# Block sums of w_up formed by GpSimd at three stretches of the front and stored, and the down stage's loads and last round in another order

## The chip, the cores and the metric

The kernel runs on one core of one Trainium2 chip. The time is the device time of one execution in microseconds (us); lower is better. Below, PE is TensorE, DVE is VectorE, ACT is ScalarE, POOL is GpSimd, and SP is SyncE, which here only issues DMAs.

## The reference

One decoder layer on x of 1024 tokens by 1024 channels, everything in float32:

```
h = RMSNorm(x);  z = h @ W_in            (pool | q | k | v | sgu u, v | three gates)
branches: pooling mixer, banded attention, chunked spatial gating, each projected to 1024
x = x + (sum_i sigmoid(gate_i) * branch_i) @ W_out
h = RMSNorm(x);  up = h @ W_up           (1024 x 5632: the first 2816 columns gate, the rest val)
up = causal depthwise conv of width 3;   x = x + (silu(gate) * val) @ W_down     (2816 x 1024)
```

The change touches the product with W_up, the product with W_down, and what runs beside the work ahead of them.

## The kernel before

**Products.** Each float32 operand is split into a high and a low part of a rounded type (fp32r): ACT copies the high part (helper line 86), DVE subtracts it from the source for the low part (line 87). One product is then three matmuls, high by high, high by low, low by high (helper `three`, lines 173 to 175). `clock` adds up the nominal time of the matmuls written so far; generators in `tasks` and similar lists are stepped as it goes on, and a scheduler of the builder then sets each engine's order from modelled durations. SP's queue of DMA issues is in order, like every engine's.

**Front (0 to about 655 us).** It runs for two halves of the tokens, t = 0 and t = 1. A half takes x in, normalises it, multiplies by the columns of W_in for keys and values, queries and gating, runs the attention, then goes through the `units` (the gated branches, whose partial sums stand in the big tile `part`), and ends with W_out. Four tiles called `x2` hold rows of x for the residual.

**Up stage (about 655 to 1103 us).** W_up's columns are taken in 22 groups c of 128 gate and 128 val columns. A group's product is made by a block scheme with seven products P1 to P7 where a plain 2 by 2 scheme has eight. The halves of the input dimension and the gate and val columns give the blocks a11, a12 (gate) and a21, a22 (val). The weights of P3, P5, P6 and P7 are sums of blocks: s1 = a21+a22 (P5), s2 = s1-a11 (P6), s3 = a11-a21 (P7), s4 = a12-s2 (P3). `up_prep` loads g and v of a group (512 KB each) into `raw` slots, POOL forms the four sums in two `q` slots (lines 858 to 861, four operations of 128x512 each), and ACT and DVE split each of the seven weights. For groups 0 to 6 P1 and P2 are done early (set PRE) and the other five products (REST) in the up stage; groups 7 to 21 do all seven there (FULL). The evacuation of a group (conv, silu, gate by val) runs on DVE and ACT, its long operation being line 875 (128x1023). The `q` slots (13 of 128x1024) are shared by sums, split weights and evacuation.

**Down stage (about 1103 us to the end).** The 22 groups are taken as 11 pairs q, in two parts (q 0 to 5, then 6 to 10), again with seven products each by blocks A11 to A22 of the gated activations (`gd`, in DRAM) and B11 to B22 of W_down. `fetch` loads the blocks of a part in a written order. Each product has four PSUM banks (i = 0 to 3); `evacuate` combines them on DVE and ACT, either at the product's last step or later (list `late`, one product on). Finished tiles are added into `out` in DRAM by accumulating DMAs that POOL issues (`add`, line 1045); the last product's tiles are stored by SP (line 1080). In the last part the order of products ends P7, P5, P4, and P5 releases eight tiles (v2 and v3, four each) to `add`. In this stage the orders of DVE and ACT are as written.

Of the kernel before, what the change touches and what calls it, by code (L numbers as in the profile page):

```python
# [35 lines left out]
LOADS, READY = 9, 7  # L36


def trunk_kernel(tc, x, positions, norm1, w_in, q_norm, k_norm, sinks, w_pool, pool_scale,
# [105 lines left out]

    def tick():
        again = True
# [22 lines left out]

    def three(ps, a, b, first, last, n=T):

        pe.matmul(ps, a(0), b(0), start=first, stop=False)  # L173
        pe.matmul(ps, a(0), b(1), start=False, stop=False)  # L174
        r = pe.matmul(ps, a(1), b(0), start=False, stop=last)  # L175
        clock[0] += 3 * n * 0.216 / 512
        return r
# [427 lines left out]

    def up_early(c):
# [33 lines left out]
    gd = [dp.tile([P, S], F32, name=f"gd{c}") for c in range(NC_FF)]  # L640
    mark = [None]
    spawn(setup_rest(), 24)
    st = Stream(w_in, 768, 256, KD, normed.ins)
    for t in range(2):
# [31 lines left out]
        part = slot("part", 1, [P, KD, T], F32)  # L676
# [34 lines left out]
        for i, c0 in enumerate(units):  # L711
            if i + 1 < len(units):
                wn = w_gran(w_in, units[i + 1])
            else:
                x2t = [slot("x2" if t == 0 else "x", 4, [P, D], F32) for _ in range(NT)]
# [31 lines left out]
        ss = slot("ssx", 2, [P, 32], F32)[:, 0:8]  # L747
        if t == 0:
# [88 lines left out]
    def up_prep(c, names):  # L837


        ws = wss[c, names]  # L840
        g = up_raw(0, c)
# [6 lines left out]
        v = up_raw(1, c)  # L848
# [5 lines left out]
        a11, a12, a21, a22 = g[:, 0:HK, :], g[:, HK:, :], v[:, 0:HK, :], v[:, HK:, :]  # L854
        sa, sb = q_([P, 2, HK, P]), q_([P, 2, HK, P])
        s1, s2, s3, s4 = sa[:, 0], sa[:, 1], sb[:, 0], sb[:, 1]
        yield
        pool.tensor_tensor(s1, a21, a22, ALU.add)  # L858
        pool.tensor_tensor(s2, s1, a11, ALU.subtract)
        pool.tensor_tensor(s3, a11, a21, ALU.subtract)  # L860
        pool.tensor_tensor(s4, a12, s2, ALU.subtract)
        for n in names:
            wt = slot("w", 4, [P, 2, HK, P], F32R) if n in ("P1", "P6", "P2") else q_([P, 2, HK, P], F32R)
            ws[n] = up_split({"P1": a11, "P2": a12, "P3": s4, "P4": a22, "P5": s1, "P6": s2, "P7": s3}[n], wt)
# [118 lines left out]
    ORDERS = ("P1", "P2", "P6", "P3", "P7", "P4", "P5"), ("P1", "P2", "P6", "P3", "P7", "P5", "P4")  # L983
# [17 lines left out]
    def fetch(a, b):  # L1001
        for j, q in enumerate(range(a, b)):
            raws[q] = slot("hh", 2, [P, 8, T], F32) if j in (0, 2) else h_([P, 8, T])
            load(q, (A11, B11, A12, B21))
        for q in range(a, b):
            load(q, (A21, B12, A22, B22))
# [40 lines left out]
    def evacuate(part, p, i, ps):  # L1047


        state = states[part]  # L1050
        s, v2, v3, p3 = (state[n][i] for n in ("s", "v2", "v3", "p3"))
        over = lambda v: dve.scalar_tensor_tensor(v, v, -1.0, ps, ALU.mult, ALU.add)
# [8 lines left out]
        elif p == "P3":  # L1061
# [130 lines left out]
```

## Time and profile before

| | us |
|---|---|
| median of 3 runs | 1324.67 (1323.91 to 1326.77) |
| the profiled execution, own time | 1327.64 |
| its span | 1325.9 |
| PE busy | 1285.3 |
| DVE busy | 974.4 |
| ACT busy | 607.8 |
| POOL busy | 189.5 |

The profiled execution is 2.97 us above the median; 1.74 us of its time lie outside the span. Busy shares are means over stages: PE is at 97%, so what can be gained is in the stretches where it is not.

### The profile page before, as it was taken

How to read it: one execution, taken by the hardware profiler on the slowest of the kernel's cores; microseconds unless marked ns; L12 is line 12 of the kernel's file. 1: busy time of each engine (PE TensorE's matmuls, PEld its weight loads, DVE VectorE, ACT ScalarE, POOL GpSimd, SP SyncE). 2: the span in 40 equal slices, each digit the busy share in tenths (PEclk: the TensorE clock that was granted, in tenths of full speed). 3: DMA queues.
4: the chain of work that ended last, by engine and by line, in shares of the span. 5: the costliest groups of instructions: out<-in, count | busy, mean ns of one | idle time of the engine just before them, and what ended most of it. 6: DMA issues, size and time to landing. Idle time of an engine off the chain costs nothing.

```text
span 1325.9 us, 16088 instructions
## 1 busy us (share of the span) xinstructions
PE 1285.3 (97%) x5956; PEld 1064.1 (80%) x5956; DVE 974.4 (73%) x1520; ACT 607.8 (46%) x990; POOL 189.5 (14%) x123
## 2 busy tenths in 40 slices
PE   6999999999999999999999999999999998999996
PEld 6888888888888888888777878878778787788885
DVE  6887875644569776355585889889998885986986
ACT  5655554333465455333573444344444343444441
POOL 0000000000000000000005454245443400101202
PEclk9999999999999999999998999999999999999999
DMA  6422224422432222533554323333232256238705
GB/s 233 118 87 64 80 80 143 115 75 94 148 118 64 81 80 79 152 113 111 200 169 139 104 71 112 112 96 111 81 111 95 80 185 243 48 107 248 122 0 96
DMA packets 167644, 151.25 MB, mean 114 GB/s; under 512 B 7615, under 2 KB 132493, under 8 KB 167565
## 3 DMA queue, kind: packets, MB, share of 16 engines
q1 hardware_dynamic: 163533, 142.87, 33.9%
q0 software_dynamic: 4032, 7.34, 3.7%
q8 instruction: 47, 0.77, 0.2%
q14 instruction: 32, 0.26, 0.1%
HBM read 120.30 MB, written 29.88 MB: 113 GB/s over the span
## 4 chain that ended last, share of the span: by engine, by line
issue 53%; PE 19%; DVE 14%; DMA 5%; ACT 4%; POOL 0%; SPq 0%; POOLq 0%; DVEq 0%; ACTq 0%
DVE x L875 6%; PE bk L1129 4%; PE bk L1128 4%; PE bk L1130 4%; DVE q L87 3%; DMA raw<-in_w_up_dram 3%; PE bk L898 2%; PE bk L899 2%; PE bk L900 2%; ACT x L871 2%; DMA hq<-in_w_down_dram 1%; DVE w L87 1%; ACT w L86 1%; ACT x L883 1%; DVE x L87 1%
## 5 line engine op out<-in xcount | busy, mean ns | idle before, releaser
L175 PE MATMUL mm<-hh,w 128*128 128x512 f32 x416 | 162.6, 391 | 0.0
L173 PE MATMUL mm<-hh,w 128*128 128x512 f32 x416 | 162.6, 391 | 0.0
L174 PE MATMUL mm<-hh,w 128*128 128x512 f32 x416 | 162.4, 390 | 0.0
L87 DVE TENSOR_TENSOR w<-raw,w 128x1024 fp32r<-128x1024 f32 (+1 forms) x96 | 93.3, 976 | 89.5 <-ACT w L86 89.5
L858 POOL TENSOR_TENSOR q<-raw 128x512 f32<-128x512 f32 x22 | 35.6, 1617 | 847.4 <-DVE w L87 653.0
L86 ACT ACTIVATE w<-raw 128x1024 fp32r<-128x1024 f32 (+1 forms) x96 | 82.3, 858 | 155.8 <-PE mm L174 67.1
L875 DVE SCALAR_TENSOR_TENSOR x<-q,cA,x 128x1023 f32<-128x1023 f32 x88 | 136.2, 1554 | 22.8 <-ACT x L871 22.3
L898 PE MATMUL bk<-hq,q 128*128 128x512 f32 x352 | 139.2, 396 | 6.1 <-DVE sm L916 5.9
L899 PE MATMUL bk<-hq,q 128*128 128x512 f32 x352 | 138.0, 392 | 0.0
L900 PE MATMUL bk<-hq,q 128*128 128x512 f32 x352 | 137.6, 391 | 0.0
L1129 PE MATMUL bk<-x,w 128*128 128x512 f32 x308 | 121.1, 393 | 2.5 <-DVE x L87 2.5
L1130 PE MATMUL bk<-w,x 128*128 128x512 f32 x308 | 120.6, 392 | 0.0
L1128 PE MATMUL bk<-w 128*128 128x512 f32 x308 | 93.4, 391 | 4.1 <-ACT w L86 3.8
L174 PEld LDWEIGHTS mm<-hh,w 128*128 128x128 f32 x416 | 78.1, 188 | 16.1
L175 PEld LDWEIGHTS mm<-hh,w 128*128 128x128 f32 x416 | 78.1, 188 | 16.1
L173 PEld LDWEIGHTS mm<-hh,w 128*128 128x128 f32 x416 | 78.1, 188 | 15.7
L87 DVE TENSOR_TENSOR wa<-raw,wa 128x512 fp32r<-128x512 f32 x72 | 49.5, 695 | 55.5 <-ACT wa L86 55.5
L898 PEld LDWEIGHTS bk<-hq,q 128*128 128x128 f32 x352 | 66.6, 189 | 24.4 <-DVE sm L916 8.5
L871 ACT ACTIVATE x<-q,cA 128x1024 f32<-128x1024 f32 x44 | 54.0, 1241 | 68.7 <-DVE q L926 38.0
L86 ACT ACTIVATE wa<-raw 128x512 fp32r<-128x512 f32 x72 | 45.2, 631 | 79.5 <-PE mm L175 67.2
L900 PEld LDWEIGHTS bk<-hq,q 128*128 128x128 f32 x352 | 66.7, 189 | 14.0
L899 PEld LDWEIGHTS bk<-hq,q 128*128 128x128 f32 x352 | 66.7, 189 | 13.7
(267 smaller groups left out, 2957.6 us busy)
## 6 DMA issues: line engine op xcount, KB each, us to landing
raw<-in_w_in_dram SPq DMA_DIRECT2D x72, 512.0 KB, 3.8
raw<-in_w_up_dram SPq DMA_DIRECT2D x51, 512.0 KB, 5.2
gd<-x SPq DMA_DIRECT2D x22, 512.0 KB, 2.8
x<-in_x_dram SPq DMA_DIRECT2D x16, 512.0 KB, 4.0
raw<-in_w_out_dram SPq DMA_DIRECT2D x16, 512.0 KB, 3.7
hq<-gd SPq DMA_DIRECT2D x28, 256.0 KB, 5.3
hq<-in_w_down_dram SPq DMA_DIRECT2D x28, 256.0 KB, 5.6
raw<-in_w_proj_b_dram SPq DMA_DIRECT2D x32, 128.0 KB, 2.7
```

Of the source, the lines that this page charges most:

```text
L86: split.last = act.activation(hi, src, AF.Copy).ins
L87: dve.tensor_tensor(lo, src, f(hi), ALU.subtract)
L173: pe.matmul(ps, a(0), b(0), start=first, stop=False)
L174: pe.matmul(ps, a(0), b(1), start=False, stop=False)
L175: r = pe.matmul(ps, a(1), b(0), start=False, stop=last)
L875: dve.scalar_tensor_tensor(y[:, n:], u[:, 0 : S - n], col(w), y[:, n:], ALU.mult, ALU.add)
L898: pe.matmul(ps, ws[n][:, 0, k, :], rhs[n](0, k), start=start and k == 0, stop=False, skip_group_check=True)
L899: pe.matmul(ps, ws[n][:, 0, k, :], rhs[n](1, k), start=False, stop=False, skip_group_check=True)
L900: pe.matmul(ps, ws[n][:, 1, k, :], rhs[n](0, k), start=False, stop=k == HK - 1, skip_group_check=True)
L1128: pe.matmul(ps[i], hi[:, 0, ts], hi[:, 1, :], start=start, stop=False, skip_group_check=True)
L1129: pe.matmul(ps[i], hi[:, 0, ts], lo[:, 1, :], start=False, stop=False, skip_group_check=True)
L1130: pe.matmul(ps[i], lo[:, 0, ts], hi[:, 1, :], start=False, stop=q == b - 1, skip_group_check=True)
```

## The change

1. A new helper `weight_sums` loads g and v of a group, lets POOL form the four sums in place (a22 becomes s1, a21 becomes s3, a11 becomes s2, a12 becomes s4) and has POOL store both tiles to a DRAM scratch `s_d[c]`. It is written as side work at three places: groups 0 to 5 from unit 16 of t = 0 on, in the four `x2` tiles; groups 6 to 13 behind the units of t = 0, in the tile `part`; and groups 14 to 21 from unit 13 of t = 1 on, in the `x2` tiles. The rows of x that stood in `x2` are loaded again later.
2. `up_prep` no longer sums. It loads the four sums from `s_d` (1 MB in two DMAs) into the two `q` slots, of v only a22 (256 KB), and g only for the groups that do P1 and P2 there.
3. `fetch` takes A11 and B11 of all q of a part first, then A12 and B21, then the rest; `hh` slots go to the first two q.
4. In the last part the order of products is P1 P2 P6 P7 P5 P3 P4. P5 finishes and adds v3, P3 (whose product is now taken straight from PSUM into v2) finishes and adds v2, and the addition of s into `o` stands two q into P3.

```diff
@@ -34,6 +34,8 @@
 N_PRE = 7
 PRE_SETS = ((0, 1), (2, 3), (4, 5, 6))
 LOADS, READY = 9, 7
+SUM_SETS = (range(0, 6), range(6, 14), range(14, 22))
+SUM_GAPS = (8.2, 8.6, 8.2)
...
@@ -603,6 +618,54 @@
         split(wt[:, 0], wt[:, 1], src)
         return wt
+    def weight_sums(cs, tiles, gap):
+        def take(c):
+            vg = tiles()
+            for o, dst in zip((1, 0), vg):
+                c0 = o * D_FF + c * P
+                with tc.issue_after(last_pe[0].ins):
+                    sp.dma_start(dst, w_up[:, c0 : c0 + P].rearrange("(k p) c -> p k c", p=P))
+            return vg
+        nxt = take(cs[0])
+        yield gap
+        for j, c in enumerate(cs):
+            v, g = nxt
+            a11, a12, a21, a22 = g[:, 0:HK], g[:, HK:], v[:, 0:HK], v[:, HK:]
+            with tc.issue_after(last_pe[0].ins):
+                pool.tensor_tensor(a22, a21, a22, ALU.add)
+            pool.tensor_tensor(a21, a11, a21, ALU.subtract)
+            pool.dma_start(s_d[c][:, 1], v)
+            pool.tensor_tensor(a11, a22, a11, ALU.subtract)
+            pool.tensor_tensor(a12, a12, a11, ALU.subtract)
+            pool.dma_start(s_d[c][:, 0], g)
+            yield gap / 2
+            if j + 1 < len(cs):
+                nxt = take(cs[j + 1])
+                yield gap / 2
...
+    def side_work(cs, tiles, gap):
+        side_line.append([clock[0], weight_sums(cs, tiles, gap)])
+    def side_end():
+        while side_line:
+            side_step()
...
@@ -709,9 +772,15 @@
         wp = None
         for i, c0 in enumerate(units):
+            if i == (16 if t == 0 else 13):
+                side_work(SUM_SETS[2 * t], own_tiles, SUM_GAPS[2 * t])
+            if i == 2:
+                side_end()
+                part = slot("part", 1, [P, KD, T], F32)
             if i + 1 < len(units):
                 wn = w_gran(w_in, units[i + 1])
             else:
+                side_end()
                 x2t = [slot("x2" if t == 0 else "x", 4, [P, D], F32) for _ in range(NT)]
                 for b in range(NT):
                     r = t * T + b * P
...
@@ -746,6 +815,12 @@
             step(tasks[0])
         ss = slot("ssx", 2, [P, 32], F32)[:, 0:8]
         if t == 0:
+            side_work(SUM_SETS[1], part_tiles(), SUM_GAPS[1])
+        else:
+            for b in range(NT):
+                x2[0][b] = slot("x2", 4, [P, D], F32)
+                sp.dma_start(x2[0][b], out[b * P : (b + 1) * P, :])
+        if t == 0:
             h = new_h()
             spawn(h_flip(1, h), 0.1)
         else:
...
@@ -836,32 +911,33 @@
     def up_prep(c, names):
         ws = wss[c, names]
-        g = up_raw(0, c)
+        if names != REST:
+            g = up_raw(0, c)
         if names == PRE:
             yield
             for n, a in (("P1", g[:, 0:HK, :]), ("P2", g[:, HK:, :])):
                 ws[n] = up_split(a, slot("w", 4, [P, 2, HK, P], F32R))
                 yield
             return
-        v = up_raw(1, c)
+        v = raw([P, HK, P])
+        c0 = D_FF + c * P
+        sp.dma_start(v, w_up[T:, c0 : c0 + P].rearrange("(k p) c -> p k c", p=P))
         if names == REST:
             st = held.setdefault(c, {})
             st["s"], st["ug"] = sm2(), q_([P, S])
             sp.dma_start(st["s"], pre_d[c][:, 0, :])
             sp.dma_start(st["ug"][:, 0:T], pre_d[c][:, 1, :])
-        a11, a12, a21, a22 = g[:, 0:HK, :], g[:, HK:, :], v[:, 0:HK, :], v[:, HK:, :]
+        yield
         sa, sb = q_([P, 2, HK, P]), q_([P, 2, HK, P])
-        s1, s2, s3, s4 = sa[:, 0], sa[:, 1], sb[:, 0], sb[:, 1]
-        yield
-        pool.tensor_tensor(s1, a21, a22, ALU.add)
-        pool.tensor_tensor(s2, s1, a11, ALU.subtract)
-        pool.tensor_tensor(s3, a11, a21, ALU.subtract)
-        pool.tensor_tensor(s4, a12, s2, ALU.subtract)
+        sp.dma_start(sa, s_d[c][:, 0].rearrange("p (j k) c -> p j k c", j=2))
+        sp.dma_start(sb, s_d[c][:, 1].rearrange("p (j k) c -> p j k c", j=2))
+        ab = {"P3": sa[:, 1], "P4": v, "P5": sb[:, 1], "P6": sa[:, 0], "P7": sb[:, 0]}
+        if names == FULL:
+            ab["P1"], ab["P2"] = g[:, 0:HK, :], g[:, HK:, :]
         for n in names:
             wt = slot("w", 4, [P, 2, HK, P], F32R) if n in ("P1", "P6", "P2") else q_([P, 2, HK, P], F32R)
-            ws[n] = up_split({"P1": a11, "P2": a12, "P3": s4, "P4": a22, "P5": s1, "P6": s2, "P7": s3}[n], wt)
+            ws[n] = up_split(ab[n], wt)
             yield
     def conv(u, c):
...
@@ -980,7 +1056,7 @@
     A11, A21, A12, A22, B11, B12, B21, B22 = range(8)
     parts = ((0, 6), (6, 11))
-    ORDERS = ("P1", "P2", "P6", "P3", "P7", "P4", "P5"), ("P1", "P2", "P6", "P3", "P7", "P5", "P4")
+    ORDERS = ("P1", "P2", "P6", "P3", "P7", "P4", "P5"), ("P1", "P2", "P6", "P7", "P5", "P3", "P4")
     SUMS = {("P1", 4): 0, ("P1", 5): 1, ("P2", 1): 2, ("P2", 2): 3, ("P2", 4): 4, ("P2", 5): 5}, \
            {("P1", 3): 0, ("P1", 4): 1, ("P2", 1): 2, ("P2", 2): 3, ("P2", 4): 4}
     raws, sums, srcs, ops, states = {}, {}, {}, {}, [{}, {}]
...
@@ -1000,10 +1076,11 @@
     def fetch(a, b):
         for j, q in enumerate(range(a, b)):
-            raws[q] = slot("hh", 2, [P, 8, T], F32) if j in (0, 2) else h_([P, 8, T])
-            load(q, (A11, B11, A12, B21))
-        for q in range(a, b):
-            load(q, (A21, B12, A22, B22))
+            raws[q] = slot("hh", 2, [P, 8, T], F32) if j < 2 else h_([P, 8, T])
+            load(q, (A11, B11))
+        for which in ((A12, B21), (A21, B12, A22, B22)):
+            for q in range(a, b):
+                load(q, which)
     def presum(q):
         r = raws[q]
...
@@ -1058,26 +1138,30 @@
             add(i, 0, o)
         elif p == "P6":
             dve.tensor_tensor(v2, s, ps, ALU.add)
-        elif p == "P3":
-            act.activation(p3, ps, AF.Copy)
         elif p == "P7":
             v3 = state["v3"][i] = sm2()
             dve.tensor_tensor(v3, s, ps, ALU.add)
-            dve.tensor_tensor(v3, v3, p3, ALU.add)
+            if not last:
+                dve.tensor_tensor(v3, v3, state["p3"][i], ALU.add)
+        elif p == "P3" and not last:
+            act.activation(state["p3"][i], ps, AF.Copy)
+        elif p == "P5" and last:
+            over(v3)
+            add(NT + i, 1, v3)
+        elif p == "P3":
+            over(v2)
+            add(i, 1, v2)
         elif p == "P5":
             for ti, v in ((i, v2), (NT + i, v3)):
                 over(v)
                 add(ti, 1, v)
-            if part + 1 == len(parts):
-                o = state["o"][:, i, :]
-                dve.tensor_tensor(o, o, s, ALU.add)
-        elif part + 1 < len(parts):
-            dve.tensor_tensor(s, s, ps, ALU.add)
-            add(NT + i, 0, s)
-        else:
+        elif last:
             o = state["o"][:, i, :]
             dve.tensor_tensor(o, o, ps, ALU.add)
             sp.dma_start(out[(NT + i) * P : (NT + i + 1) * P, 0:T], o)
+        else:
+            dve.tensor_tensor(s, s, ps, ALU.add)
+            add(NT + i, 0, s)
     def olds():
...
@@ -1129,15 +1215,19 @@
             pe.matmul(ps[i], hi[:, 0, ts], lo[:, 1, :], start=False, stop=False, skip_group_check=True)
             pe.matmul(ps[i], lo[:, 0, ts], hi[:, 1, :], start=False, stop=q == b - 1, skip_group_check=True)
             if q == b - 1:
-                if p == "P1" or p == "P4" and part + 1 == len(parts) or p == "P7" and part + 1 < len(parts):
+                if p in (("P1", "P6", "P5", "P4") if last else ("P1", "P7")):
                     evacuate(part, p, i, ps[i])
                 else:
                     late.append((part, p, i, ps[i]))
         if p == "P4" and q == a:
             if part + 1 < len(parts):
                 fetch(*parts[part + 1])
-        if p == "P7" and q == a and part + 1 == len(parts):
+        if last and q == a and p == "P7":
             olds()
+        if last and q == a + 2 and p == "P3":
+            for i in range(NT):
+                o = state["o"][:, i, :]
+                dve.tensor_tensor(o, o, state["s"][i], ALU.add)
```

POOL's whole order at the start of the front, before. `sm_103` holds the spatial gating's weights, whose upper triangle line 342 clears; the `raw` and `q` names are the first group's blocks and sums in the up stage.

```order
L300 MEMSET kT 128x4x128
L301 MEMSET hist 128x32
L342 AFFINE_SELECT sm_103_711<-sm_103_711 128x512
L858 TENSOR_TENSOR q_5989<-raw_5987 128x512
L860 TENSOR_TENSOR q_5990<-raw_5985,raw_5987 128x512
L859 TENSOR_TENSOR q_5989<-q_5989,raw_5985 128x512
L861 TENSOR_TENSOR q_5990<-raw_5985,q_5989 128x512
```

The same place after; `x_317` to `x_416` are the `x2` tiles of groups 0 to 4, `ws_256` to `ws_260` their scratch in DRAM.

```order
L316 MEMSET hist 128x32
L638 TENSOR_TENSOR x_317_2094<-x_317_2094 128x512
L639 TENSOR_TENSOR x_317_2094<-x_318_2095,x_317_2094 128x512
L640 DMA ws_256<-x_317_2094 128x1024
L641 TENSOR_TENSOR x_318_2095<-x_317_2094,x_318_2095 128x512
...
L642 TENSOR_TENSOR x_390_2482<-x_390_2482 128x512
L643 DMA ws_259<-x_390_2482 128x1024
L357 AFFINE_SELECT sm_103_733<-sm_103_733 128x512
L639 TENSOR_TENSOR x_415_2639<-x_416_2640,x_415_2639 128x512
L640 DMA ws_260<-x_415_2639 128x1024
```

The clearing of the triangle, which was POOL's first work in the front, now stands behind four groups of sums and the first sum of a fifth. From line 858 on nothing of POOL's sums is left in the up stage.

SP's queue early in the front, before, from its row 18 on. `raw` names are blocks of W_in, `x2_409` to `x2_412` rows of x.

```order
L312 DMA sink_t_229<-in_sinks_dram 128x8 [waits DMAHW1_49]
L718 DMA x2_409_2608<-in_x_dram 128x1024 [waits DMAHW2_49]
L718 DMA x2_410_2609<-in_x_dram 128x1024 [waits DMAHW3_49]
L718 DMA x2_411_2610<-in_x_dram 128x1024 [waits DMAHW4_49]
L718 DMA x2_412_2611<-in_x_dram 128x1024 [waits DMAHW5_49]
L233 DMA raw_64_462<-in_w_in_dram 128x2x512 [waits DMAHW6_49,DVE_49]
L233 DMA raw_67_494<-in_w_in_dram 128x2x512 [waits DMAHW7_49,DVE_49]
L233 DMA raw_72_548<-in_w_in_dram 128x2x512 [waits DMAHW0_49,DVE_49]
L233 DMA raw_76_584<-in_w_in_dram 128x2x512 [waits DMAHW6_49,DMAHW1_49,DVE_49]
```

The same place after.

```order
L327 DMA sink_t_229<-in_sinks_dram 128x8 [waits DMAHW1_49]
L629 DMA x2_317_2094<-in_w_up_dram 128x8x128 [waits DMAHW2_49]
...
L248 DMA raw_64_484<-in_w_in_dram 128x2x512 [waits DMAHW6_49,DVE_49]
L248 DMA raw_67_516<-in_w_in_dram 128x2x512 [waits DMAHW7_49,DVE_49]
L629 DMA x2_363_2323<-in_w_up_dram 128x8x128 [waits DMAHW0_49,DMAHW2_49,DMASW0_49,Pool_49]
L248 DMA raw_72_570<-in_w_in_dram 128x2x512 [waits DMAHW1_49,DVE_49]
L629 DMA x2_364_2324<-in_w_up_dram 128x8x128 [waits DMAHW3_49,DMASW1_49,Pool_49]
L629 DMA x2_389_2481<-in_w_up_dram 128x8x128 [waits DMAHW4_49,DMASW2_49,Pool_49]
L248 DMA raw_76_606<-in_w_in_dram 128x2x512 [waits DMAHW6_49,DVE_49]
```

Groups 0 and 1 load where x was loaded, so their sums begin at the front's start although the code writes them at unit 16; from group 2 on a load in SP's queue waits for POOL and for POOL's store (DMASW) of the group two before, with blocks of W_in behind it.

DVE's last rows before. `sm_1612` to `sm_1615` are v3, `hq_9902` the four tiles of v2, `hq_10319` the four of o, `x` names the low parts of the products' operands.

```order
L87 TENSOR_TENSOR x_10481<-hq_9684,w_10480 128x1024
L1052 SCALAR_TENSOR_TENSOR hq_9902<-hq_9902,bk_10203 128x512
L1052 SCALAR_TENSOR_TENSOR sm_1612_10392<-sm_1612_10392,bk_10203 128x512
L1073 TENSOR_TENSOR hq_10319<-hq_10319,hq_9902 128x512
...
L87 TENSOR_TENSOR x_10517<-hq_9689,w_10516 128x1024
L1079 TENSOR_TENSOR hq_10319<-hq_10319,bk_10103 128x512
L1079 TENSOR_TENSOR hq_10319<-hq_10319,bk_10104 128x512
```

DVE's last rows after; v3 is `sm_1626` to `sm_1629`, v2 `hq_10079`, o `hq_10401`.

```order
L1131 SCALAR_TENSOR_TENSOR sm_1626_10478<-sm_1626_10478,bk_10470 128x512
...
L89 TENSOR_TENSOR x_10608<-hh_9846,w_10607 128x1024
L1230 TENSOR_TENSOR hq_10401<-hq_10401,hq_10079 128x512 x4
L89 TENSOR_TENSOR x_10628<-hh_9849,w_10627 128x1024
...
L1131 SCALAR_TENSOR_TENSOR hq_10079<-hq_10079,bk_10470 128x512
...
L89 TENSOR_TENSOR x_10684<-hq_9858,w_10683 128x1024
L1160 TENSOR_TENSOR hq_10401<-hq_10401,bk_10280 128x512
```

v3 is finished one whole product earlier than v2, the additions of s into o stand in the middle of P3, and only v2's four tiles are finished in the last product.

## Rows read from the trace of the kernel before

**Rows 1.** The page, part 1: busy us by engine, share, instructions.

```profile
PE 1285.3 (97%) x5956; PEld 1064.1 (80%) x5956; DVE 974.4 (73%) x1520; ACT 607.8 (46%) x990; POOL 189.5 (14%) x123
```

**Rows 2.** Windows, up stage to down stage: start:end, length, busy us (instructions) per engine.

```profile
core 0: us, PE busy (x) PEld busy (x) DVE busy (x) ACT busy (x) POOL busy (x), PEclk, DMA share, GB/s
700.00:800.00 100.00, 96.17 (x410) 78.20 (x409) 82.26 (x87) 41.37 (x63) 48.23 (x28) 0.97 0.34 104
800.00:900.00 100.00, 97.77 (x428) 79.64 (x427) 88.17 (x91) 43.23 (x61) 44.15 (x24) 1.00 0.31 96
900.00:1000.00 100.00, 97.80 (x429) 79.99 (x428) 88.81 (x93) 42.08 (x59) 40.21 (x21) 1.00 0.34 106
1000.00:1050.00 50.00, 48.98 (x215) 39.92 (x214) 46.07 (x48) 21.44 (x31) 21.59 (x12) 1.00 0.34 105
1050.00:1100.00 50.00, 50.00 (x222) 41.41 (x221) 39.77 (x42) 21.30 (x26) 8.47 (x4) 1.00 0.50 173
```

**Rows 3.** Waits of PE, 640 to 1326: total us, times, longest us.

```profile
PE bk L898 <- DVE sm L916: 5.9, 6, 1.8
PE bk L898 <- ACT w L86: 4.4, 2, 3.2
PE bk L1128 <- ACT w L86: 3.8, 1, 3.8
PE bk L1128 <- DVE sm L1065: 0.4, 1, 0.4
```

**Rows 4.** POOL's sums, line 860: ns min/median/max, first and last start us.

```profile
L860 POOL TENSOR_TENSOR q<-raw,raw x22: 1273/2273/2287, 702.1 to 1055.8; 128x512 f32<-128x512 f32 x22
```

**Rows 5.** Groups of DVE instructions: busy us, mean ns of one, idle before.

```profile
L875 DVE SCALAR_TENSOR_TENSOR x<-q,cA,x 128x1023 f32<-128x1023 f32 x88 | 136.2, 1554 | 22.8 <-ACT x L871 22.3
L87 DVE TENSOR_TENSOR q<-q,q 128x512 fp32r<-128x512 f32 x66 | 66.8, 1021 | 8.4 <-ACT q L86 8.3
L87 DVE TENSOR_TENSOR q<-raw,q 128x512 fp32r<-128x512 f32 x22 | 27.9, 1270 | 0.0
```

**Rows 6.** DVE on tiles q, 700 to 1100: ns min/median/max.

```profile
L875 DVE SCALAR_TENSOR_TENSOR x<-q,cA,x x84: 1275/1285/2357, 731.1 to 1089.7; 128x1023 f32<-128x1023 f32 x42, 128x1022 f32<-128x1022 f32 x42
L87 DVE TENSOR_TENSOR q<-q,q x66: 676/686/1780, 704.1 to 1077.7; 128x512 fp32r<-128x512 f32 x66
L928 DVE SCALAR_TENSOR_TENSOR q<-sm,bk x21: 673/680/684, 732.3 to 1084.8; 128x512 f32<-128x512 f32 x21
```

**Rows 7.** Windows of three stretches of the front, columns as in rows 2.

```profile
18.00:73.00 55.00, 55.00 (x313) 47.66 (x312) 42.10 (x90) 30.44 (x50) 1.18 (x1) 1.00 0.47 146
285.00:345.00 60.00, 60.00 (x320) 51.46 (x320) 26.93 (x41) 23.38 (x45) 0.00 (x0) 1.00 0.34 114
345.00:430.00 85.00, 84.42 (x424) 70.84 (x423) 65.62 (x156) 48.44 (x88) 0.00 (x0) 1.00 0.31 91
```

**Rows 8.** POOL's clearing of the triangle (timeline), and its reader on PE (line 346).

```profile
46.64 1.18 POOL L342 TENSOR_SCALAR_AFFINE_SELECT sm<-sm 128x512 f32<-128x512 f32 x1 [45.24 <-DMA sm<-in_w_pool_dram]
...
L346 PE MATMUL at<-cA,sm x4: 271/272/274, 59.8 to 60.2; 128*128 128x128 f32 x4
```

**Rows 9.** A load of the front on SP, and its first use on PE (timeline).

```profile
70.03 0.37 SPq L614 DMA_DIRECT2D raw<-in_w_proj_a_dram  x1
...
103.82 0.39 PE L173 MATMUL mm<-x,wp 128*128 128x512 f32 x1
```

**Rows 10.** The page, part 6: DMA issues, KB each, us from issue to landing.

```profile
raw<-in_w_up_dram SPq DMA_DIRECT2D x51, 512.0 KB, 5.2
gd<-x SPq DMA_DIRECT2D x22, 512.0 KB, 2.8
```

**Rows 11.** The first split that ACT makes of the down stage's last pair (timeline).

```profile
1112.91 1.06 ACT L86 ACTIVATE w<-hq 128x1024 fp32r<-128x1024 f32 x1 [8.11 <-DMA hq<-in_w_down_dram]
```

**Rows 12.** The end: last matmul, last accumulating DMA, stores (timeline: start, length us).

```profile
1315.54 0.40 PE L1130 MATMUL bk<-w,x 128*128 128x512 f32 x1
...
1317.92 0.88 POOL L1045 DMA_DIRECT2D out_dram<-sm  x1 [0.93 <-DVE hq L1079]
...
1315.29 2.93 SPq L1080 DMA_DIRECT2D out_dram<-hq  x4
```

More of the change, by code (lines that the diff above doesn't have):

```diff
@@ L144, in trunk_kernel, with side_step @@
     tasks = []
+    side_line = []
+    def side_step():
+        try:
+            side_line[0][0] = clock[0] + next(side_line[0][1])
+        except StopIteration:
+            side_line.pop(0)
     def tick():
+        while side_line and side_line[0][0] <= clock[0]:
+            side_step()
         again = True
@@ L168, in need @@
             step(tk)
+    last_pe = [None]
     def three(ps, a, b, first, last, n=T):
@@ L174, in three @@
         pe.matmul(ps, a(0), b(1), start=False, stop=False)
-        r = pe.matmul(ps, a(1), b(0), start=False, stop=last)
+        r = last_pe[0] = pe.matmul(ps, a(1), b(0), start=False, stop=last)
         clock[0] += 3 * n * 0.216 / 512
@@ L604, in up_split, with own_tiles, part_tiles, tiles @@
         return wt
+    def weight_sums(cs, tiles, gap):
[22 more added lines that the diff above has]
+                yield gap / 2
+    def own_tiles():
+        return [slot("x2", 4, [P, KD, P], F32) for _ in range(2)]
+    def part_tiles():
+        big = slot("part", 1, [P, 4, KD, P], F32)
+        turn = [0]
+        def tiles():
+            turn[0] ^= 2
+            return big[:, turn[0]], big[:, turn[0] + 1]
+        return tiles
+    def side_work(cs, tiles, gap):
+        side_line.append([clock[0], weight_sums(cs, tiles, gap)])
+    def side_end():
+        while side_line:
+            side_step()
     def up_early(c):
@@ L640, in trunk_kernel @@
     gd = [dp.tile([P, S], F32, name=f"gd{c}") for c in range(NC_FF)]
+    s_d = [dp.tile([P, 2, KD, P], F32, name=f"ws{c}") for c in range(NC_FF)]
     mark = [None]
@@ L675, in trunk_kernel @@
         tick()
-        part = slot("part", 1, [P, KD, T], F32)
         mxs = [lambda q, m=m: m[:, q, :] for m in mx]
@@ L1047, in evacuate, with over @@
     def evacuate(part, p, i, ps):
-        state = states[part]
-        s, v2, v3, p3 = (state[n][i] for n in ("s", "v2", "v3", "p3"))
-        over = lambda v: dve.scalar_tensor_tensor(v, v, -1.0, ps, ALU.mult, ALU.add)
+        state, last = states[part], part + 1 == len(parts)
+        s, v2, v3 = (state[n][i] for n in ("s", "v2", "v3"))
+        def over(v):
+            dve.scalar_tensor_tensor(v, v, -1.0, ps, ALU.mult, ALU.add)
         if p == "P1":
@@ L1102, in trunk_kernel @@
         a, b = parts[part]
-        start = q == a and p in ("P1", "P6", "P3")
+        last = part + 1 == len(parts)
+        key = "P1" if p in ("P1", "P2") else "P6" if p in ("P6", "P7", "P4") else "P5" if last else "P3"
+        start = q == a and p == key
         if start:
@@ L1112, in trunk_kernel @@
                 states[part]["p3"] = [t[:, h, :] for t in (q_([P, 2, T]) for _ in range(2)) for h in range(2)]
-        ps = sets["P1" if p in ("P1", "P2") else "P6" if p in ("P6", "P7", "P4") else "P3"]
+        ps = sets[key]
         if j + ahead + 1 < len(todo):
```

## The prediction

> **What bounds the kernel now.** The page comes first: PE is busy for 97% of the span, POOL for 14% [rows 1]. A gain can only come from stretches in which PE is not at its full rate, so the windows come next. From 1050 to 1100 PE starts 222 matmuls in 50 us, 0.225 us each, and is not idle at all: that is the full rate. By it 444 would start in 100 us. The windows of the up stage fall short of it by 34, 16, 15 and 7 [rows 2], which is 72 x 0.225 = 16.2 us. In the same windows DVE is busy for 305.3 of 350 us and POOL for 154.2, and once POOL's sums are over (1050 to 1100, POOL 8.47 us) PE is whole again. So the up stage is held back by what feeds it, while the sums run. The waits of PE say by what: in lines 898 to 900 it waits 5.9 us for DVE's evacuations and 4.4 us for ACT's splits of weights [rows 3]; the rest is many short starts that come late and are no wait of their own.
>
> DVE is slower there than its work asks. The operation of line 875 takes 1.285 us in the median and up to 2.357; line 87 on `q` tiles 0.686 and up to 1.780; line 928, which reads PSUM, stays between 0.673 and 0.684 [rows 6]. POOL's sums show the counterpart, 1.273 us at least and 2.273 in the median [rows 4]. Over all of them the means are 1.554, 1.021 and 1.270 us [rows 5] where the least is 1.275, 0.676 and 0.676 [rows 6]: 88 x 0.279 + 66 x 0.345 + 22 x 0.594 = 24.6 + 22.8 + 13.1 = 60.5 us of DVE time are lost to 88 sums, 0.69 us for each. The Trainium skill says why (SBUF — State Buffer, section "SBUF: two separate sides"): DVE and GpSimd share a pair of ports under an exclusive lock, and an operation of DVE with two SBUF inputs and one of GpSimd that reads SBUF block one another for a whole instruction; the unslowed line 928 agrees.
>
> **The change part by part.**
>
> *Sums out of the up stage.* 88 sums go, and with them up to 60 of DVE's 305 us in those windows, so that DVE stands near 70%. At most all the starvation goes, 16.2 us. At least the waits for ACT's splits go, since a weight no longer waits for a chain of four sums before it can be split: 4.4 us, less what the new loads bring back; I set that bound at 3. What speaks for the low end is that sa and sb are now loaded by SP into the same shared `q` slots, in order, and their loads wait for PE, DVE and ACT to release them, as POOL's writes did. A 512 KB load lands 5.2 us after issue [rows 10], where a chain of four sums took 4 x 2.27 = 9.1 us, so a late load still comes earlier than a late chain. More bytes are no bound: a FULL group moves 1.75 MB (g, a22 and four sums) for 1 MB, so 15 x 0.75 + 7 x 0.25 = 13 MB over some 400 us are 33 GB/s on top of 104, at a DMA share of a third [rows 2]. I take -12, as three quarters of the shortfall, since DVE's own order (5.9 us) is only eased: **-12, from -3 to -16**.
>
> *Sums into the front.* The order shows where they run, and it is not where the code writes them: the first set starts where x was loaded, some 12 to 18 us into the kernel. By the order the three stretches hold 24, 28 and 36 sums (the last group of the second set runs among the third), about 18 to 73, 285 to 345 and 345 to 430 us. PE has no gap in the first two and 0.6 us in the third, so every delay that reaches it counts; what hides the sums is DVE's idle time, 55 - 42.1 = 12.9, 60 - 26.9 = 33.1 and 85 - 65.6 = 19.4 us [rows 7]. No sum ran there before, so the price per sum is bounded: below nothing, where DVE happens to have other inputs or a gap; above the whole 1.273 us of a sum [rows 4]. At 0.69 us, the price of the up stage, DVE gets 16.6, 19.3 and 24.8 us more, and overshoots its idle time by 3.7, 0 and 5.4, in sum 9.1 us. At 1.273 it gets 30.6, 35.6 and 45.8, and overshoots by 17.7, 2.5 and 26.4, in sum 46.6. I stay near the price that was measured, and take two thirds of its 9.1, since DVE may catch up behind a stretch: **+6, from 0 to 47**. Without the cover of idle time, 88 x 0.69 would be 61 us.
>
> *What the sums are queued ahead of.* On POOL the clearing of the triangle (line 342) now stands behind 17 sums and eight stores. It ran at 46.6 us and PE reads its result at 59.8 [rows 8]: 12 us of slack. Seventeen sums of 1.273 us from some 18 us on end at 40; at 2.27 they end at 57, and the reader is late by nothing to a few us. On SP the loads of groups 2 to 5 wait for POOL's sums and stores, with blocks of W_in behind them. Loads on SP are far ahead of use: one issued at 70.0 is first read by PE at 103.8 [rows 9], and a wait of a sum pair and a store (2 x 1.273 + 2.8 = 5.4 us, the landing taken from the page [rows 10]) is within that. I cost both at 0, and at 4 us together if the sums run at the slow price; that is part of the upper bound above. The reloads of x into `x2` come before their reader in a stretch in which loads land in 4 to 5 us: 0.
>
> *The order of the loads.* The transition from up to down stage waits 3.8 us for one split [rows 3], of the last pair, whose source lands at 1112.9 after 8.1 us in which ACT waits [rows 11]. In the new order A11 and B11 of all pairs are written first, but the last pair's first load stands 42nd in the fetch in both orders, since its slot is released by PE late, and the queue moves as many bytes before it. The best that earlier loads could give is the stretch's wait, so **0, from -4 to 0**.
>
> *The last round.* Before, the last matmul starts at 1315.54, the last accumulating DMA is issued by POOL from 1317.92 for 0.88 us, and the span ends at 1325.9 [rows 12]: 10 us after PE. P5's eight tiles meet POOL's queue at about one issue in 1.5 us, in the last product's time. After, v3's four adds lie one product earlier and only v2's four lie in the last one, early in it. The end is then the last product's own: one evacuation (0.68 us, as line 928 [rows 6]), one issue on SP (2.93 / 4 = 0.73) and a landing (2.8, as the 512 KB store `gd` [rows 10]), about 4 us behind PE in place of 10: -6. Against it, P6 and P5 now free their banks at once, where a later product's first matmul waits: the one such wait in the trace is 0.4 us [rows 3], two of them about 1. **-5, from -2 to -6.**
>
> *Sum.* -12 + 6 + 0 - 5 = -11 us on the profiled execution's 1327.64, so 1316.6; that execution is 2.97 above the median of the runs, so the median should be **1313.5**.
>
> **The rivals.**
>
> *The front hides all, and the up stage gets all back.* For it: DVE has 65 us idle in the three stretches, and the first two have no gap in PE that shows a tight feed [rows 7]. Against it: the third has 0.6 us already. -16 - 5 = -21: 1303.5.
>
> *The up stage stays starved.* The `q` slots, not the sums, would be what is short: POOL's chain only filled the time until a slot was free, and now SP waits for the slot, with g and a22 of the next group behind it in its queue. For it speaks that the 5.9 us of waits for DVE come from the order of the evacuation and not from weights [rows 3]; against it that DVE loses up to 1.1 us in a clash [rows 6]. -3 + 6 - 5 = -2: 1322.7, no change that can be told from zero.
>
> *Slower: DVE blocked by sums in the front.* In the first and third stretch each sum may hold DVE for longer than the 0.69 us of the up stage, because there the DVE's work is short splits with two SBUF inputs, which all clash, while in the up stage part of it reads PSUM. It decides from the price at which the overshoot eats the 17 us gained: 24p - 12.9 + 36p - 19.4 = 17 gives p = 0.82 us per sum. Halfway from there to 1.273, at 1.05, the overshoot is 12.3 + 18.4 = 30.7, less 17: 1338.4; at 1.273 it is 46.6 less 17: 1354. By the lock in the Trainium skill (SBUF — State Buffer, "SBUF: two separate sides") a sum that starts first blocks such an operation for up to its whole length, which would be that upper price. For the rival: the longest line 87 lost 1.1 us [rows 6]. Against it: the mean loss in the up stage, where POOL was busy for almost half of the time, was 0.69.
>
> **How the numbers follow.** The measurement can tell about 0.2% from no change, 2.65 us. The likeliest case (1313.5, its own range 1306 to 1320) gets 0.50, the full gain 0.16, the starved up stage 0.14, the slower case 0.20. The range of all reaches from just under the full gain, 1301, to 1330, which takes in the third case and the lower end of the slower one, and leaves out some 0.17, nearly all above. Faster by over 0.2%: 0.49 + 0.16 + 0.05 of the third case = 0.70; within: 0.09; slower: 0.20 and 0.01 of the first, 0.21.
>
> **What the profile after would show.** If right: no POOL sums between 650 and 1100, line 875 at 1.28 us in the mean, and PE at 435 or more matmuls per 100 us there; DVE busy for some 52 to 55 of 55 us in the first stretch and PE short by about 20 matmuls over the first and third; the wait of ACT at the transition unchanged near 8 us; 4 to 5 us between last matmul and end of span. It would be wrong if the `q` loads show up as releasers of ACT's splits in the up stage; if PE waits for line 87's low parts between 18 and 73 or 345 and 430 for more than 10 us, or for the cleared triangle; or if the granted clock falls behind such a stall, since these stretches run at 1.00 now [rows 7].

## The result, and the profile after

The change made the kernel slower: 1370.18 us (median of 4 runs, 1369.77 to 1371.58) against 1325.72, a ratio of 1.0339 with a 95% interval of 1.0325 to 1.0352. The profiled execution took 1370.21 us, its span is 1368.5.

Where the 42.6 us of span lie is read from PE's timeline, since both kernels run the same 5956 matmuls. Here is the first matmul of the up stage and of the down stage before (start, length); the last one is in [rows 12]:

```profile
653.84 0.47 PE L898 MATMUL bk<-hh,w 128*128 128x512 f32 x1
...
1088.34 0.62 PE L1128 MATMUL bk<-w 128*128 128x512 f32 x2
```

After, the same two and the last:

```profile
710.67 0.47 PE L974 MATMUL bk<-hh,w 128*128 128x512 f32 x1
...
1129.53 0.62 PE L1214 MATMUL bk<-w 128*128 128x512 f32 x2
...
1363.34 0.39 PE L1216 MATMUL bk<-w,x 128*128 128x512 f32 x1
```

| us | front | up stage | down stage to its last matmul | behind it |
|---|---|---|---|---|
| before | 653.8 | 434.5 | 227.2 | 10.4 |
| after | 710.7 | 418.9 | 233.8 | 5.2 |
| difference | +56.9 | -15.6 | +6.6 | -5.2 |

The windows of after, columns as in [rows 2]; the first three hold nearly the work of those in [rows 7] (312, 314 and 421 matmuls for 313, 320 and 424):

```profile
18.00:90.00 72.00, 61.45 (x312) 52.37 (x312) 64.26 (x89) 30.45 (x49) 42.53 (x37) 0.95 0.84 260
307.00:367.00 60.00, 58.88 (x314) 50.15 (x312) 35.44 (x40) 23.16 (x45) 33.77 (x32) 1.00 0.82 259
367.00:486.00 119.00, 94.77 (x421) 75.14 (x419) 101.14 (x148) 46.31 (x79) 68.66 (x60) 0.90 0.84 264
760.00:860.00 100.00, 100.00 (x443) 82.86 (x442) 72.25 (x93) 45.40 (x64) 0.00 (x0) 1.00 0.45 143
860.00:960.00 100.00, 100.00 (x443) 82.86 (x442) 76.46 (x96) 45.01 (x61) 0.00 (x0) 1.00 0.42 134
```

The up stage is whole: PE starts 443 matmuls in 100 us, the full rate. The first stretch takes 17 us longer for nearly the same matmuls and the third 34; the second loses little, and some 5 us lie outside the three. Not all of the 51 us are idle time of PE. Its granted clock, 1.00 in the first and third stretch before, is 0.95 and 0.90 there: behind its waits PE runs for a while at the lower of its two levels, 1.2 GHz. PE idles 10.6 and 23.7 us more in the two stretches, and it is busy for 6.5 and 10.4 us more for these matmuls. By the granted clock the lower rate can be 3.6 of the 6.5 us (0.05 of 72 us) and all of the 10.4 (0.10 of 119 us is 11.9). So some 34 of the 51 us are added waits, and up to 14 are the clock behind them.

DVE is busy for 22.2, 8.5 and 35.5 us more in the three stretches, and yet has 7.7 and 17.9 us idle in the first and third. Next come groups of DVE instructions (busy us, mean ns of one, idle before). The first is the split of W_in's and W_out's weights in tile `wa`, before:

```profile
L87 DVE TENSOR_TENSOR wa<-raw,wa 128x512 fp32r<-128x512 f32 x72 | 49.5, 695 | 55.5 <-ACT wa L86 55.5
```

and after, with two groups that answer to [rows 5]:

```profile
L89 DVE TENSOR_TENSOR wa<-raw,wa 128x512 fp32r<-128x512 f32 x72 | 73.9, 1039 | 54.0 <-ACT wa L88 54.0
...
L951 DVE SCALAR_TENSOR_TENSOR x<-q,cA,x 128x1023 f32<-128x1023 f32 x88 | 112.0, 1279 | 19.2 <-ACT x L947 18.7
...
L89 DVE TENSOR_TENSOR q<-q,q 128x512 fp32r<-128x512 f32 x66 | 45.1, 686 | 15.7 <-ACT q L88 15.7
```

What the up stage's operations lost (1554 and 1021 ns before) is gone, and `wa` lost instead. Its median is still 0.69 us; a few of the 72 are very long, the longest 6.2 us. PE's largest waits from 340 to 500 us (total us, times, longest us) name the same split:

```profile
PE mm L189 <- DVE wa L89: 9.1, 5, 4.2
PE mm L188 <- ACT wa L88: 6.1, 1, 6.1
```

The first is for DVE's low part. The second is for ACT's high part of the same split, and ACT had itself waited for a load there; its line stands further down, with the loads.

This is how one operation loses: DVE, and below it POOL, at 44 us (timeline: start, length).

```profile
43.42 0.68 DVE L89 TENSOR_TENSOR wa<-raw,wa 128x512 fp32r<-128x512 f32 x1
44.03 3.85 DVE L131 SCALAR_TENSOR_TENSOR rs<-rs 128x8 f32<-128x8 f32 x1
47.80 0.68 DVE L89 TENSOR_TENSOR wa<-raw,wa 128x512 fp32r<-128x512 f32 x1
...
44.08 1.30 POOL L641 TENSOR_TENSOR x<-x,x 128x512 f32<-128x512 f32 x1
45.33 1.28 POOL L638 TENSOR_TENSOR x<-x 128x512 f32<-128x512 f32 x1
46.59 1.26 POOL L642 TENSOR_TENSOR x<-x 128x512 f32<-128x512 f32 x1
48.14 0.57 POOL L643 DMA_DIRECT2D ws<-x  x1 [0.30 <-POOL x L642]
```

An operation of 8 columns, one of a chain of small ones (line 131 has a median of 0.16 us), stands for 3.85 us while three sums run one behind the other, and the next split of `wa` stands behind it.

In the last part of the down stage PE waits twice; DVE and PE are shown at the second wait.

```profile
PE bk L1214 <- DVE hq L1140: 2.1, 1, 2.1
PE bk L1214 <- DVE sm L1131: 1.9, 1, 1.9
...
1331.54 1.22 DVE L1104 TENSOR_TENSOR hq<-hq,q 128x1024 f32<-128x1024 f32 x1
1332.68 1.22 DVE L89 TENSOR_TENSOR x<-hq,w 128x1024 fp32r<-128x1024 f32 x1
1333.81 2.47 DVE L1131 SCALAR_TENSOR_TENSOR sm<-sm,bk 128x512 f32<-128x512 f32 x4
...
1334.64 0.47 PE L1214 MATMUL bk<-w 128*128 128x512 f32 x1 [1.88 <-DVE sm L1131]
...
1336.21 0.63 PE L1216 MATMUL bk<-w,x 128*128 128x512 f32 x1
```

P3 adds into the banks in which P5 ended, so its first matmul needs P5's evacuation, and DVE has a difference and a split of 1.22 us each queued ahead of that. Behind this wait some matmuls take 0.63 us instead of 0.39; the granted clock is 0.57 from 1335 to 1339 us, after 1.00 from 1300 to 1335.

### The profile page after: what moved, and what is told of

It reads as the page before. It is cut to its first block, busy times and chain, and to the rows that moved or that the text cites. A ratio compares the mean times of both kernels' runs of the same rounds, so it can differ in the third digit from the quotient of the medians.

```text
span 1368.5 us, 16329 instructions
## 1 busy us (share of the span) xinstructions
PE 1300.4 (95%) x5956; PEld 1074.3 (79%) x5956; DVE 987.2 (72%) x1516; ACT 608.9 (44%) x986; POOL 176.2 (13%) x167
## 5 line engine op out<-in xcount | busy, mean ns | idle before, releaser
L89 DVE TENSOR_TENSOR w<-raw,w 128x1024 fp32r<-128x1024 f32 (+1 forms) x96 | 97.4, 1017 | 69.6 <-ACT w L88 69.5
L951 DVE SCALAR_TENSOR_TENSOR x<-q,cA,x 128x1023 f32<-128x1023 f32 x88 | 112.0, 1279 | 19.2 <-ACT x L947 18.7
L89 DVE TENSOR_TENSOR wa<-raw,wa 128x512 fp32r<-128x512 f32 x72 | 73.9, 1039 | 54.0 <-ACT wa L88 54.0
L1122 POOL DMA_DIRECT2D out_dram<-sm x16 | 14.2, 1013 | 748.0 <-ACT sm L1137 701.9
L1214 PE MATMUL bk<-w 128*128 128x512 f32 x308 | 96.6, 395 | 8.4 <-ACT w L88 2.9
L189 PE MATMUL mm<-wa,hh 128*128 128x512 f32 (+1 forms) x192 | 73.8, 386 | 17.8 <-DVE wa L89 17.7
L975 PEld LDWEIGHTS bk<-hq,q 128*128 128x128 f32 x352 | 66.1, 188 | 13.7
L974 PEld LDWEIGHTS bk<-hq,q 128*128 128x128 f32 x352 | 66.1, 188 | 13.7
```

The source lines that it names most:

```text
L89: dve.tensor_tensor(lo, src, f(hi), ALU.subtract)
L951: dve.scalar_tensor_tensor(y[:, n:], u[:, 0 : S - n], col(w), y[:, n:], ALU.mult, ALU.add)
L974: pe.matmul(ps, ws[n][:, 0, k, :], rhs[n](0, k), start=start and k == 0, stop=False, skip_group_check=True)
L975: pe.matmul(ps, ws[n][:, 0, k, :], rhs[n](1, k), start=False, stop=False, skip_group_check=True)
L1214: pe.matmul(ps[i], hi[:, 0, ts], hi[:, 1, :], start=start, stop=False, skip_group_check=True)
```

## The experiments

Theory A says that POOL's sums block DVE's operations in the front, and that chains of DVE on which PE depends hang on these. Its rivals are B, the new loads and stores fill the DMA engines and SP's queue, and C, DVE has simply no time there for more work. A further question is the place. Each time below is a median in us, with the median of the kernel before on the same chip and the interval of the ratio; "front" is the start of the up stage's first matmul in the profiled execution, against 653.8.

| run | us | before | ratio (95%) | front |
|---|---|---|---|---|
| e1_as_written | 1344.84 | 1323.76 | 1.0148 to 1.0185 | +38.5 |
| e2_no_sums | 1319.18 | 1323.76 | 0.9942 to 0.9974 | +10.5 |
| e3_no_loads | 1376.64 | 1323.76 | 1.0376 to 1.0429 | +67.2 |
| e4_down_only | 1322.51 | 1323.76 | 0.9977 to 0.9994 | +1.9 |
| e5_units_only | 1310.96 | 1324.79 | 0.9883 to 0.9918 | -0.3 |
| e6_down_fixed | 1317.14 | 1324.79 | 0.9930 to 0.9955 | -0.1 |
| e7_dve_sums | 1352.24 | 1324.79 | 1.0182 to 1.0221 | +39.5 |
| e8_memsets | 1322.93 | 1324.79 | 0.9977 to 0.9999 | +13.2 |
| e9_units_fixed | 1307.30 | 1323.38 | 0.9855 to 0.9896 | -0.1 |
| e10_gaps | 1362.80 | 1323.38 | 1.0268 to 1.0320 | +50.8 |
| e11_waits | 1368.14 | 1326.28 | 1.0308 to 1.0348 | +54.9 |

**Without the sums (e2).** The four `pool.tensor_tensor` and their `issue_after` are left out of `weight_sums`, so the kernel stores plain blocks.

> The changed kernel with its loads and stores of the front, but without POOL's 88 sums (what is stored are the plain blocks, so the up stage multiplies other weights). Theory A (DVE blocked by the sums makes the front's loss): of the 57 us at most 15 are left, 1313 to 1328. Theory B (the loads and stores make it, by the DMA engines and by SP's queue): 40 or more are left, 1353 to 1370.

The front loses 10.5 us instead of 56.9, and `wa` is back at its old length:

```profile
L89 DVE TENSOR_TENSOR wa<-raw,wa 128x512 fp32r<-128x512 f32 x72 | 49.2, 695 | 61.7 <-ACT wa L88 61.7
```

So about 46 us come with the sums and 10 are what the loads and stores cost by themselves.

**Without the loads (e3).** Each set loads its first two groups and sums the same tiles again for the others. Shown is the first part of the edit; in the second the first and third set take two pairs of `x2` tiles in turn.

```diff
             vg = tiles()
+            if c - cs[0] >= 2:
+                return vg
```

> The changed kernel with its sums and stores of the front, but each set loads only its first two groups and sums the same tiles again for the others (32 of 44 loads left out, so the sums are of other blocks). Theory A (DVE blocked by the sums): 35 or more of the 57 us are left, 1348 to 1370. Theory B (loads): at most 20 are left, 1313 to 1333.

This is worse than the change itself: with nothing to wait for, the sums follow one another more densely. Theory B is out as the main cause. DVE, and below it POOL, at 380 us:

```profile
380.56 0.16 DVE L138 TENSOR_SCALAR rs<-ss 128x8 f32<-128x8 f32 x1
380.75 8.44 DVE L127 TENSOR_SCALAR rs<-rs 128x8 int32<-128x8 int32 x1
...
381.09 1.30 POOL L643 TENSOR_TENSOR x<-x,x 128x512 f32<-128x512 f32 x1
...
386.08 1.26 POOL L644 TENSOR_TENSOR part<-part 128x512 f32<-128x512 f32 x1
387.28 0.58 POOL L645 DMA_DIRECT2D ws<-x  x1
387.88 1.27 POOL L641 TENSOR_TENSOR x<-x,x 128x512 f32<-128x512 f32 x1
```

POOL runs six sums and one issue in these 8.44 us.

**Memsets for sums (e8).** Each `pool.tensor_tensor(d, ...)` becomes `pool.memset(d, 0.01)`.

> The changed kernel with POOL's 88 sums replaced by as many memsets of the same tiles, in the same order (no sum is formed, the up stage gets constants). If POOL blocks DVE by reading two operands beside it, the loss goes as it did without sums: 1316 to 1326. If any operation of POOL on these tiles blocks DVE, it stays in proportion to the memsets' length: 1335 to 1370.

```profile
L639 POOL MEMSET x<- x14: 519/526/668, 19.4 to 433.0; 128x512 f32 x14
...
L89 DVE TENSOR_TENSOR wa<-raw,wa 128x512 fp32r<-128x512 f32 x72 | 49.4, 696 | 62.7 <-ACT wa L88 62.6
```

The first row is the length of a memset (ns min/median/max), the second DVE's group. A memset is 0.41 of a sum in length. If any operation of POOL on these tiles blocked DVE, some 19 of the 46 us would in proportion be left above e2, and 2.7 are. So POOL's instructions on these tiles hardly block DVE as such; those that read operands do.

**DVE makes the sums (e7).** `pool.tensor_tensor` becomes `dve.tensor_tensor` in `weight_sums`.

> The changed kernel with its 88 sums of the front made by DVE, in the same places, in place of POOL. Theory A (POOL's sums block single operations of DVE for longer than the work is worth): a sum costs DVE 0.68 us and blocks nothing, 60 us against 65 of idle time, so the front loses 10 (its loads) to 25: 1325 to 1343. Theory C (DVE simply has no time left there, and POOL only takes it as DVE would): 1355 to 1375.

The front loses 39.5 us, and the time lies between the two expectations. C is part of it: 88 more operations on DVE, some 60 us, cost 29 us above e2, though DVE's idle time in the three stretches, 65 us, was larger than they are. But the same sums on the idle engine cost 17 us more than on the busy one. So of the 46 us about 29 would come from DVE's time alone, and 17 from POOL's blocking on top of it.

**The places (e1, e5).** One element of each `x2` tile is first written by ACT from the last unit's tile, so the load can't run ahead of that unit. Shown is the write alone.

```diff
+                if anchor[0] is not None:
+                    act.activation(dst[:, 0, 0:1], anchor[0][:, 0:1], AF.Copy)
                 with tc.issue_after(last_pe[0].ins):
```

> The changed kernel, with one element of each x2 tile copied by ACT from the tile th of the last unit before its load is issued, so that the first and third set of sums can't start before the units at which the code writes them (about 205 and 500 us). Theory of place (sums cost where DVE is busy or loads are dense, and next to nothing where DVE is half idle): the front's loss of 57 us falls to 3 to 10, and the time to 1312 to 1322. Rival (a sum costs the same wherever it runs, some 0.65 us each): 1350 to 1370.

This is a miss by over 20 us, between theory and rival. Beside the units the sums cost next to nothing: up to 290 us of the old timeline PE is not behind. The second set, beside W_out and then beside the keys and queries of t = 1, still costs about 20. And the third set now ends at 640 us, and the reload of x into `x2` comes behind it: PE loses about 10 us at W_out's splits, whose loads stand in SP's queue behind that reload, and 9 at the norm. The next run drops both; it sums 12 groups only and starts two units earlier, and the other ten groups are summed in the up stage as before (shown in part):

```diff
-SUM_SETS = (range(0, 6), range(6, 14), range(14, 22))
+SUM_SETS = (range(7, 13), (), range(13, 19))
```

> Sums moved for 12 groups only (7 to 18), six beside the units of t = 0 from unit 14 on and six beside those of t = 1 from unit 11 on, tied to their units as in the run before; the other ten groups are summed in the up stage as in the kernel before, and nothing is summed beside W_out. Theory of place: in the units DVE is half idle, so the front loses 0 to 5 us; the up stage gets back 12 of 22 of its 16, so -8.6, and the down stage -1: 1314 to 1320. Rival (each sum costs some 0.65 us anywhere): 48 sums cost 31, 1340 or more.

```profile
200.00:285.00 85.00, 85.00 (x377) 70.38 (x376) 56.83 (x98) 32.91 (x66) 38.84 (x34) 1.00 0.91 263
500.00:615.00 115.00, 115.00 (x521) 95.49 (x520) 70.03 (x111) 45.60 (x85) 31.91 (x29) 1.00 0.75 218
730.00:1035.00 305.00, 305.00 (x1347) 252.49 (x1347) 252.32 (x288) 137.17 (x189) 53.59 (x32) 1.00 0.39 128
```

These windows of e5 are the two stretches with sums and the up stage; the first two before, in the same columns:

```profile
200.00:285.00 85.00, 85.00 (x376) 70.38 (x376) 44.94 (x98) 32.75 (x57) 0.00 (x0) 1.00 0.41 124
500.00:615.00 115.00, 115.00 (x523) 95.47 (x521) 64.30 (x111) 43.93 (x73) 0.00 (x0) 1.00 0.38 112
```

DVE loses 11.9 and 5.7 us to the sums beside the units too, and PE loses nothing: it is whole in all three windows. The up stage takes 418.9 us, as in the change, although ten groups are still summed in it. That is a larger gain than the 8.6 us expected, and it brings the time to 1311; why the ten groups cost PE nothing there was not tested.

**The down stage (e4, e6).** In e4 the kernel before gets the new down stage.

> The kernel before with the down stage of the changed one (order of the loads, order of the last round). The prediction put this part at -5 us: 1319 to 1322. By the trace after, the last part loses 6.2 us at two boundaries between products and gains 5.4 behind the last matmul: 0 to +1.5, 1325 to 1328.

The time lies between the two ranges: the last part's waits (2.1 us for P6's evacuation, 1.2 for a split of ACT, and a slower rate behind the first) eat nearly all that the end gains. In e6, for the steps in which P6 and P5 end in the last part, `source` and `operands` of the look-ahead are called behind the matmuls and their evacuations (shown in part):

```diff
+        defer = last and q == b - 1 and p in ("P6", "P5")
+        if not defer:
+            prepare()
...
+        if defer:
+            prepare()
```

> The kernel before with the down stage of the changed one, and in the last part, where P6 and P5 end, the look-ahead's split and difference written behind the four evacuations and not ahead of them. Theory (two queued operations of 1.2 us each on DVE made the next product wait, 2.1 and 1.9 us, and half the rate behind it the rest): the two boundaries cost 0.4 to 0.8 each in place of 5.1 together, 1318 to 1320. Rival (the wait is for the evacuations themselves, which share the banks with the next product): 1322 to 1323, as without this edit.

The two waits are gone from PE's list, and the time is 5.4 us below e4, a little more than expected. Run e9 joins e5 and e6:

> The kernel with 12 groups summed beside the units (1311.0) and, in the last part, the look-ahead's work written behind the evacuations (which took 5.4 us off the kernel with the new down stage alone). If the two gains are in places that don't touch one another, they add: 1304 to 1308. Rival: the down stage's gain was partly the late end of its up stage: 1309 to 1312.

1307.3 us, 1.24% under the kernel before: the version to use, ahead of both kernels.

**Rows of sums (e10, e11).** These are two tries at why a sum costs more in the front than in the up stage. In e10 a memset of 128x128 is written behind each sum; in e11 each sum of a group after the first waits for a small copy by ACT, of which the first is shown:

```diff
                 pool.tensor_tensor(a22, a21, a22, ALU.add)
+            act.activation(a21[:, 0, 0:1], a22[:, 0, 0:1], AF.Copy)
```

> The changed kernel with a memset of 128x128 by POOL behind each of its 88 sums (on part of the sum's own tile, so the stored sums hold wrong values there), so that few sums follow one another without a gap in which POOL does not read. Theory A1 (an operation of DVE waits through a whole row of sums, and rows are what made a sum cost DVE 1.0 us and not 0.69): the longest operations of DVE fall from 6.2 to about 2.4 us, DVE loses 0.7 or less for each sum, and the time falls to 1335 to 1355. Rival A2 (each sum blocks for itself, rows don't matter): 1365 to 1380.

> The changed kernel in which, inside a group, each sum after the first waits for a copy of one column that ACT makes from the sum before it into the tile that the next sum reads (so one column of the stored sums is wrong). POOL then often has nothing that may run behind a sum. Theory A1 as left by the run with memsets (an operation of DVE gets in only where POOL has to wait): the longest operations of DVE fall to 3.8 us or less and a sum costs DVE 0.7 us or less; the time falls to 1335 to 1358. Rival A2 (rows don't matter to the time): 1362 or more, since ACT's 66 copies add waits.

The longest operation of `wa` fell from 6.2 to 4.4 and 5.1 us, and the mean (1039 ns in the change) did not follow. The group of e10 and then of e11:

```profile
L89 DVE TENSOR_TENSOR wa<-raw,wa 128x512 fp32r<-128x512 f32 x72 | 77.3, 1088 | 39.9 <-ACT wa L88 39.8
```

```profile
L89 DVE TENSOR_TENSOR wa<-raw,wa 128x512 fp32r<-128x512 f32 x72 | 72.8, 1022 | 58.9 <-ACT wa L88 58.9
```

The time fell by about 7 us in e10, which lies between its two ranges, and not clear of the noise in e11, which lies in the rival's. So rows of sums are not shown to make the loss. But neither edit made all the gaps that were meant: in e11 POOL waits for ACT only 16 times for 66 copies. Whether an operation of DVE gets in where POOL has to wait stays open.

## Why the prediction was wrong, by its steps

The forecast was 1313.5 (its sum gives 1313.7), the time 1370.2. The slower rival, with a chance of 0.20, had the right two stretches and half of the mechanism. Its price of 1.05 us a sum was not too low (0.92 and 0.91 were measured there), but like the forecast it counted DVE's idle time as cover, and so it came to 1338, at most 1354.

- *What bounds the up stage*: right. By the two profiles it got back 15.6 of 16.2 us where -12 was taken, and PE is whole: DVE's own order was not a floor. But the profiled execution before lies 2.97 us above its median, and its window from 700 us on ran at a granted clock of 0.97 [rows 2]. In e4 and e6, which keep the sums in the up stage, the stage takes 430.1 and 430.3 us in place of 434.5. So some 11 of the 15.6 us are the sums'; the other 4 lie in that execution or come with the new down stage, which was not separated.
- *Sums into the front, +6*: the step that failed is "what hides the sums is DVE's idle time". The DVE time that the sums add was about as forecast, 66.2 us by the windows against 60.7 at 0.69 us a sum. But it came unevenly (22.2, 8.5 and 35.5 us for 16.6, 19.3 and 24.8; 24, 22 and 39 sums ran there, so 0.92, 0.39 and 0.91 us each), and idle time did not absorb it. By the forecast's own sum the first and third stretch overshot by 9.3 and 16.1 us, while PE lost 17 and 34, since DVE was left with 7.7 and 17.9 us idle that nothing could use and PE's clock fell behind the stalls, which the forecast had named as a sign of being wrong. Idle time of an engine is cover only where the next thing that PE needs doesn't stand behind the delayed one; here the keys' and queries' chains of small operations stand ahead of the splits of `wa`. In e7, where DVE makes the sums itself and they would fit into that idle time, they still cost 29 us. In the units the same kind of sums cost PE nothing (e5).
- *Loads and stores at 0*: 10 us too low (e2). The rows that showed loads far ahead of use were from a front with a DMA share of 0.31 to 0.47 [rows 7]; with the loads and stores it is 0.82 to 0.84 in the change. Whether the DMA engines or the order of SP's queue make the 10 us was not separated. A split of ACT at 385 us in the change waits 10.87 us for a block of W_in, and PE 6.1 us behind it:

```profile
385.31 1.15 ACT L88 ACTIVATE wa<-raw 128x512 fp32r<-128x512 f32 x2 [10.87 <-DMA raw<-in_w_in_dram]
```

- *The triangle behind 17 sums at 0*: right in size, but by luck. It was cleared at 62.5 us, later than even the slow price's 57 and than the 59.8 at which PE read it before [rows 8]. No wait shows because the reader itself came 14 us later, behind the other delays:

```profile
L357 POOL TENSOR_SCALAR_AFFINE_SELECT sm<-sm x1: 1034/1034/1034, 62.5 to 62.5; 128x512 f32<-128x512 f32 x1
...
L361 PE MATMUL at<-cA,sm x4: 271/272/274, 73.8 to 74.2; 128*128 128x128 f32 x4
```

- *The transition at 0*: right in size. No split there holds PE for longer than 2.2 us now, but several shorter waits have taken the place of the one of 3.8.
- *The last round, -5*: the -6 behind the last matmul was about right (10.4 to 5.2 us). The +1 for two boundaries was mis-sized: about 6 in the change, 5 in e4. It was priced from a wait of 0.4 us [rows 3] where DVE's order has nothing ahead of the evacuation. e6 shows that the work written ahead of it was the whole difference.

## What to carry to other kernels

Work moved to an idle engine is free only if that engine doesn't hold what a busier one needs: look in the trace for the same operation at two lengths, and find the other engine's instruction beside it, before counting the idle time of either as cover. Where a scheduler may pull side work forward, read in its order where it lands, and tie it to the place with a real dependency; 12 of the 22 groups in the right place gave the whole gain. And where a product accumulates into banks that must be read first, put nothing on the evacuating engine ahead of that reading.

## What the runs showed of the hardware

The wait of a DVE operation is not bounded by one sum. In the up stage before, the longest loss was 1.1 us [rows 6]; in the front an operation of 8 columns stood for 3.85 us through three sums, and in e3 one that reads a single SBUF operand stood for 8.44 through six. POOL pays less there: the difference a11-a21 takes 1.45 us in the median in the `x2` tiles and 1.29 in `part` (line 639 of the change), where it took 2.27 in the up stage before (line 860 [rows 4]). What decides who pays is not shown. The Trainium skill (SBUF — State Buffer, section "SBUF: two separate sides") has the loser blocked for a whole instruction of the other; these rows agree that it is blocked and show more than one instruction. POOL's memsets, which read nothing, hardly slowed DVE: the splits of `wa` took 696 ns in the mean against 695 in e2, though one small operation of line 127 took 1.03 us.
